# Layer 1 of a two-layer trunk with h's hi and lo parts joined in one matmul, and the context's residual added by DMA

## The chip, the cores and the metric

The kernel runs on one core of one Trainium2 chip. The metric is the device time of one execution in microseconds (us); of several runs the median is given. The engines are TensorE (PE, matmuls; PEld is its load of weights), VectorE (DVE), ScalarE (ACT), GpSimd (POOL) and SyncE (SP), which issues the DMAs.

## The reference

Two layers (DEPTH = 2) of a hybrid mixer work on 256 latent tokens and 256 context tokens of 2048 features, batch 1, all in float32:

```python
for l in range(DEPTH):
    shift, scale, gate = jnp.split(silu_c @ w_mod[l] + b_mod[l], 3, axis=-1)      # and _c from c_ctx
    h = rmsnorm(x, g_pre[l]) * (1.0 + scale[:, None]) + shift[:, None]            # h_c from ctx
    proj, proj_c = h @ w_in[l], h_c @ w_in[l]
    # columns of proj: a_u, a_v, a_g (512 each), b_q (1024), b_k, b_v (256 each), b_g (1024), c_x, c_g (512 each)
    y_a = chunk_gmlp(gelu(a_u), gelu(a_v), ...) * silu(a_g)
    y_b = attention(b_q, b_k, b_v, context's k and v, sink) * silu(b_g)
    y_c = fourier_mix(c_x, w_f, b_f) * silu(c_g)
    x_new = x + gate[:, None] * rmsnorm(concat(y_a, y_b, y_c) @ w_out[l], g_post[l])
    if not last: ctx = ctx + gate_c * rmsnorm(y_of_ctx @ w_out[l], g_post[l])
    x = x_new
```

The output is x, the latent stream. In layer 1, the last, the context matters only through its keys and values, so of the context only the columns b_k and b_v are computed there.

## The kernel before, in words

**Exact products.** A float32 product is made of three matmuls in the format fp32r: every operand is split into hi (the value cast to fp32r, on ACT) and lo (value less hi, on DVE), and `mm3` (lines 383 to 386) adds hi·hi, hi·lo and lo·hi in PSUM. The feature-major streams are kept as 16 tiles `hh[k]` and `hl[k]` of [128 features, 512], latents in columns 0 to 255 and context in 256 to 511.

**Weights.** `Stream` (lines 329 to 379) loads w_in and w_out in pieces of [128, 1024] ("halves") through SP into a ring `raw` of three, and splits each into `whi` (ACT, line 367) and `wlo` (DVE, line 368), rings of four, ahead of their use.

**Units.** `tunit(n)` (line 473) makes 128 output columns of the projection for n tokens: 16 k steps, each three matmuls with a [128, 128] piece of the weights as the stationary operand and h as the moving one. In layer 0 n is 512, in layer 1 it is 256 (latents), and 512 for the two k units. The start of a layer makes a_v (token-major, `start_av`) and the first two heads of a_u (`start_au`) with k outermost, while h of the next k tile is being made (`prep_h`, `make_h`, lines 445 to 459). Then come the units au2, au3, cx0 to cx3, ag0 to ag3, cg0 to cg3, k0, k1, then v, q0 to q7, bg0 to bg7, and the output projection: `out_proj` feature-major in layer 0, `finish` token-major in layer 1, with four column groups c, two token tiles t and 16 k steps.

**Order.** The order on PE is the order of the program text (`manual_schedule`). Work that goes to other engines and comes back to PE is written as generators: each is queued in `later` with delays in planned us, and `later.tick` runs it when as much planned matmul time has passed (YF between the stages of the C branch, YQ, YA and YB in attention, YX, YR and YH at the boundary, YT in the output projection). DVE, ACT, POOL and SP run in an order that a scheduler makes from the program's order and priorities; `low(n)` lowers a priority. Each of these engines takes its instructions strictly in that order.

**Modulation.** Silu(c) @ w_mod is summed on DVE for most columns, in steps of two [128, 512] products per 512 KB load into the ring `mraw` of two. `RATE` says how many steps go beside each phase of units (`pace`). The last of them is layer 1's gate (`mod_gate1`, lines 236 to 252): four accumulators of [128, 512], in the tiles ctrh, ctrl, nstrh and nstrl. `gate1` (lines 254 to 263) sums each over the partitions with ones on PE and applies b_mod and g_post, whose rows come by DMA into `mraw`.

**Boundary.** Between the layers, `boundary(s, acc)` (line 908) makes x1 = x0 + gate * y / rms(y) of a stream: the sums of squares in `acc` give r; every tile is multiplied by r on DVE, x0, loaded by SP into places of the ring `raw`, is added (DVE or POOL), and ACT squares the result. PE sums the squares with ones (line 944) to get the next 1/rms. The latents go first (s = 0, at the end of layer 0). The context (s = 1, `boundary_ctx`, line 980) runs beside the units of layer 1 from au3 on, with lowered priority; it then makes the context's h, 16 tiles in the order `ORDER`.

**Places in layer 1.** `ysl(k)`, the result of a branch, lies in the context half of `yo[k]`, so a gate that writes it must come after the context's h of tile k has been made (the assertion in `gate`). Products not yet gated lie in y1: the A branch's in the tile `vv`, the C branch's in kt0 and kt1.

Of the kernel before, what the change touches and what calls it, by code (L numbers as in the profile page):

```python
# [7 lines left out]
F32 = mybir.dt.float32  # L8
# [3 lines left out]
ALU = mybir.AluOpType  # L12
# [15 lines left out]
def units():  # L28
    """(name, first column, columns, first k tile, k tiles): blocks of w_in of 128 x 2048 each."""
# [37 lines left out]
def trunk_kernel(ctx: ExitStack, tc: tile.TileContext, xT, xhalf, cT, wss, wsl, wmod, win, wout0, wout1, const, vec, rows,  # L67
# [24 lines left out]
    # ---- constants  # L92
# [17 lines left out]
    class low:  # L110
        """instructions that may wait for the next `n`."""
# [22 lines left out]
    # ---- modulation: columns [128, 16, stream] of scale, shift and gate  # L134
# [5 lines left out]
    def mod_cols(l, cb, ps8):  # L140
        """ps8 [128, 4, 2]: silu(c) @ w_mod for 512 columns of column block cb."""
# [54 lines left out]
    def mod_dve(l, cb, red):  # L196
        """red [128, 2, 16]: sums over the 32 partitions of each quadrant, transposed."""
# [38 lines left out]
    def mod_gate1():  # L236
        """products of silu(c) and the gate's columns of w_mod in layer 1, still to be summed over partitions."""
# [16 lines left out]
    def gate1():  # L254
        """(sum + b_mod) * g_post of layer 1's gate, on all partitions."""
        for c in range(4):
            r = sb([P, 2, 512], F32, "mraw", 2)
            DMA.dma_start(r, rows[None, :, c * 512:(c + 1) * 512].to_broadcast([P, 2, 512]))
            ps = ms_ps("gate")
            PE.matmul(ps, ones, g1[c], start=True, stop=True)  # L260
            V.tensor_tensor(out=g1[c], in0=r[:, 0], in1=ps, op=ALU.add)
            V.tensor_tensor(out=g1[c], in0=g1[c], in1=r[:, 1], op=ALU.mult)
            yield YT

    def mod_rest():
# [3 lines left out]
        while "acc" not in state:  # L269
# [58 lines left out]
    # ---- weights: raw -> exact parts hi + lo, in halves of a unit, ahead of their use  # L328
# [59 lines left out]
    def part(w, c):  # L388
        """columns c of both parts; a part is a tile or a list of tiles side by side."""
# [19 lines left out]
    # ---- per-token reciprocal rms from sums over features  # L409
# [14 lines left out]
    def col_sums(ps, q, n, start=True, stop=True):  # L424
        """columns of ps: sums over the partitions of q [128, n * 128], one accumulation group."""
# [10 lines left out]
    # ---- streams in feature-major tiles  # L436
# [7 lines left out]

    def make_h(l, k, rb, streams):
        """h = x * rstd * gs + sh, as hi + lo; rb: rstd over the tokens of `streams`."""
# [6 lines left out]
        for s in streams:  # L453
            sl = slice(s * S, (s + 1) * S)
            first = A.activation(hh[k][:, sl], t[:, sl], AF.Identity, bias=sh[l][:, k, s:s + 1])  # L455
        for s in streams:
            sl = slice(s * S, (s + 1) * S)
            last = V.scalar_tensor_tensor(out=hl[k][:, sl], in0=t[:, sl], scalar=sh[l][:, k, s:s + 1],
                                          in1=hh[k][:, sl].bitcast(F32), op0=ALU.add, op1=ALU.subtract)
# [13 lines left out]
    def tunit(n, sl=None):  # L473
        """feature-major product of one unit of 128 columns: PSUM [128, n]."""
# [8 lines left out]
        return ps  # L483

# [610 lines left out]
```

## Time and profile before

| | |
|---|---|
| median of 3 runs | 1171.52 us (1169.95 to 1171.75) |
| span of the profiled execution, first to last instruction | 1167.9 us; of its time around the span nothing is listed, the median of the runs is 3.6 us above it |
| PE busy | 1136.0 us (97%) |
| DVE, ACT, POOL busy | 881.8, 509.8, 17.3 us |
| mean granted TensorE clock | 0.996 |
| start (modulation and layer 0's first products) | 0 to 137 us |
| layer 0's units and output projection | 137 to 757 us |
| layer 1's start (a_v, au0, au1) | 757 to 794 us |
| au2 to cg3, beside them the context's boundary | 794 to 891 us |
| k0, k1, then v | 891 to 936 us |
| q and bg units with attention | 936 to 1062 us |
| output projection and the end | 1062 to 1168 us |

Rows of a group read: line, engine, operation, out<-in by the program's names, shapes, count, then busy time in us and mean ns of one, then the engine's idle time just before these instructions and what ended most of it. Rows of the timeline read: start in us, duration in us, engine, line, operation, names, shapes, count, and in brackets idle time before it with what ended it. Matmuls overlap, so the distance of their starts is their cost. Rows of waits read: who waited for whom, total us, times, longest us. DMA rows give the issues, KB each and the median us from issue to landing.

### The profile page before, as it was taken

The page shows a single profiled execution, that of the slowest core. Times are in us where ns is not written, and L with a number is a line of the kernel's source. Part 1 is how long each engine was busy: PE and PEld are TensorE (multiplying, and loading weights), DVE is VectorE, ACT ScalarE, POOL GpSimd, SP SyncE. Part 2 cuts the span into 40 slices and gives each one's busy share as a digit, 9 for nine tenths or more (in the row PEclk, how much of TensorE's full clock was granted, in tenths as well). Part 3 has the DMA queues.
Part 4 walks back from the last instruction along what each step waited for, and adds up shares of the span by engine and source line. Part 5 has one row for each costly group of instructions (what it writes and reads, how often), then busy time and mean ns, then how long its engine had stood idle before and what let it go on. Part 6 is the DMA issues. An engine that isn't in the chain of part 4 may idle for free.

```text
span 1167.9 us, 17483 instructions
## 1 busy us (share of the span) xinstructions
PE 1136.0 (97%) x6656; PEld 953.7 (82%) x6656; DVE 881.8 (76%) x1469; ACT 509.8 (44%) x914; POOL 17.3 (1%) x23
## 2 busy tenths in 40 slices
PE   3999999999999999999999999999999999999996
PEld 1466688888898888888888888889899999997885
DVE  5454498888988878798989886495896678888554
ACT  4222513322224667632533233365563278745442
POOL 0000000000000000000000000200000000000001
PEclk9999999999999999999999999999999999999998
DMA  9999765466665334455466665365656665688563
GB/s 339 378 387 357 254 196 166 145 202 193 200 200 178 105 114 136 134 175 173 158 199 209 205 216 162 109 207 173 205 158 205 203 200 178 195 269 244 190 187 120
DMA packets 73892, 234.32 MB, mean 201 GB/s; under 512 B 8528, under 2 KB 9680, under 8 KB 73808
## 3 DMA queue, kind: packets, MB, share of 16 engines
q1 hardware_dynamic: 73808, 233.21, 61.6%
q8 instruction: 52, 0.85, 0.3%
q14 instruction: 32, 0.26, 0.1%
HBM read 231.08 MB, written 2.10 MB: 200 GB/s over the span
## 4 chain that ended last, share of the span: by engine, by line
PE 92%; DVE 3%; DMA 2%; ACT 2%; issue 1%; POOL 0%; SPq 0%; DVEq 0%; ACTq 0%; POOLq 0%
PE ps_t L384 20%; PE ps_t L385 20%; PE ps_t L386 20%; PE ps_mod L172 3%; PE ps_av L384 2%; PE ps_y L386 2%; PE ps_y L384 2%; PE ps_y L385 2%; PE ps_av L385 2%; PE ps_av L386 2%; PE ps_v L386 1%; PE ps_v L384 1%; PE ps_v L385 1%; PE ps_tp L722 1%; PE ps_au L384 1%
## 5 line engine op out<-in xcount | busy, mean ns | idle before, releaser
L384 PE MATMUL ps_t<-hh,whi 128*128 128x512 f32 (+1 forms) x1296 | 452.1, 349 | 0.0
L386 PE MATMUL ps_t<-hh,wlo 128*128 128x512 f32 (+1 forms) x1296 | 447.4, 345 | 0.0
L385 PE MATMUL ps_t<-hl,whi 128*128 128x512 f32 (+1 forms) x1296 | 447.0, 345 | 0.0
L367 ACT CAST whi<-raw 128x1024 fp32r<-128x1024 f32 x218 | 228.2, 1050 | 397.3 <-PE ps_t L385 274.4
L368 DVE TENSOR_TENSOR wlo<-raw,whi 128x1024 fp32r<-128x1024 f32 x218 | 265.3, 1220 | 99.1 <-ACT whi L367 98.8
L384 PEld LDWEIGHTS ps_t<-hh,whi 128*128 128x128 f32 x1296 | 244.9, 189 | 34.3 <-issue 4.6
L386 PEld LDWEIGHTS ps_t<-hh,wlo 128*128 128x128 f32 x1296 | 244.7, 189 | 30.6
L385 PEld LDWEIGHTS ps_t<-hl,whi 128*128 128x128 f32 x1296 | 244.9, 189 | 28.9 <-issue 0.5
L209 DVE SCALAR_TENSOR_TENSOR macc<-mraw,cs,macc 128x512 f32<-128x512 f32 x360 | 249.9, 745 | 17.6 <-DMA mraw<-in_wmod_dram 17.5
L455 ACT ACTIVATE hh<-w2k,sh 128x256 fp32r<-128x256 f32 x64 | 29.0, 502 | 61.4 <-DVE w2k L451 61.4
L384 PE MATMUL ps_y<-whi,hh 128*128 128x512 f32 x112 | 45.0, 401 | 0.0
L386 PE MATMUL ps_y<-whi,hl 128*128 128x512 f32 x112 | 43.8, 392 | 0.0
L385 PE MATMUL ps_y<-wlo,hh 128*128 128x512 f32 x112 | 43.7, 390 | 0.0
L384 PE MATMUL ps_av<-whi,hh 128*128 128x512 f32 x96 | 40.0, 416 | 0.0
L385 PE MATMUL ps_av<-wlo,hh 128*128 128x512 f32 x96 | 37.9, 395 | 0.4 <-DVE wlo L368 0.4
L172 PE MATMUL ps_mod<-hh,kt 128*32 128x512 f32 x64 | 21.5, 649 | 17.0 <-DMA hh<-in_wss_dram 17.0
L386 PE MATMUL ps_av<-whi,hl 128*128 128x512 f32 x96 | 37.6, 392 | 0.0
L386 PE MATMUL ps_v<-whi,hl 128*128 128x256 f32 x128 | 36.2, 283 | 0.0
L384 PE MATMUL ps_v<-whi,hh 128*128 128x256 f32 x128 | 36.2, 283 | 0.0
L385 PE MATMUL ps_v<-wlo,hh 128*128 128x256 f32 x128 | 36.2, 283 | 0.0
L468 DVE TENSOR_TENSOR acc<-acc,w2k 128x512 f32<-128x512 f32 (+1 forms) x33 | 21.2, 641 | 18.7 <-ACT w2k L467 17.2
L401 ACT CAST w2k<-ps_tp 128x512 fp32r<-128x512 f32 x40 | 23.5, 587 | 22.8 <-PE ps_scc L385 12.0
(292 smaller groups left out, 1491.8 us busy)
## 6 DMA issues: line engine op xcount, KB each, us to landing
raw<-in_win_dram SPq DMA_DIRECT2D x160, 512.0 KB, 4.1
mraw<-in_wmod_dram SPq DMA_DIRECT2D x128, 512.0 KB, 4.3
raw<-in_wout_dram SPq DMA_DIRECT2D x64, 512.0 KB, 4.2
hh<-in_wss_dram SPq DMA_DIRECT2D x32, 256.0 KB, 5.6
hl<-in_wss_dram SPq DMA_DIRECT2D x32, 256.0 KB, 5.4
yo<-in_xT_dram SPq DMA_DIRECT2D x16, 256.0 KB, 5.4
mraw<-in_wsl_dram SPq DMA_DIRECT2D x8, 512.0 KB, 6.9
yo<-in_wsl_dram SPq DMA_DIRECT2D x16, 256.0 KB, 7.2
```

The lines of the kernel that those rows point to most:

```text
L172: PE.matmul(ps[32 * kk:32 * kk + 32, 0:n], cpad[:, kg * 4 + kk], ws[kk], start=kg == 0, stop=kg == 3, tile_position=(0, 32 * kk))
L209: V.scalar_tensor_tensor(out=acc[:, s], in0=w[:, kk % 2], scalar=c, in1=acc[:, s], op0=ALU.mult, op1=ALU.add)
L367: A.copy(ph, r[:, c])
L368: self.last = V.tensor_tensor(out=pl, in0=r[:, c], in1=ph.bitcast(F32), op=ALU.subtract)
L384: PE.matmul(ps, st[0], mv[0], start=start, stop=False)
L385: PE.matmul(ps, st[0], mv[1], start=False, stop=False)
L386: PE.matmul(ps, st[1], mv[0], start=False, stop=stop)
L401: A.copy(hi, src)
L455: first = A.activation(hh[k][:, sl], t[:, sl], AF.Identity, bias=sh[l][:, k, s:s + 1])
L468: V.tensor_tensor(out=acc[:, sl], in0=acc[:, sl], in1=q[:, sl], op=ALU.add)
L722: PE.transpose(tp[:, (2 * j + b) * P:(2 * j + b + 1) * P], src, ident)
```

## The change

Five edits, all in layer 1 or at the boundary to it; the program of layer 0 stays as it is.

1. *Joined parts.* In layer 1 `hh[k]` holds the latents' h as [hi | lo], 512 columns, and `hl[k]` the context's in the same way. A k step of a latent unit is then two matmuls (`mm2`): the weights' hi with all 512 columns, the weights' lo with the 256 columns of hi, into one bank of PSUM. `joined` adds the two halves of the result: an ACT copy of one out of PSUM, a DVE addition of the other, into a tile of the ring `join` of two. The k units do this for both streams with two banks. What followed a unit (gates, rope, the C branch, gelu) reads the joined tile.
2. *Context's x0 by DMA.* `boundary_ctx` multiplies a tile by r on DVE, and then POOL issues a DMA that adds x0 from DRAM to it. Squares come six tiles later (LATE), on ACT; they are added up on DVE into acc, and the sums over the partitions are made at the end by the same few products as the first ones.
3. *A longer chain.* The context's h is made in the order 12 to 15, then 0 to 11, and planned delays change (YF of layer 1 from 3.8 and 3.4 to 6.0 and 5.2; YC, YE new).
4. *y of branch A apart.* The results of ag0 to ag3 stay in y1, now in the tile `macc`, so their gates no longer wait for the context's h.
5. *Gate sums at fixed places.* `gate1(c)` is called at four places of the output projection (GATES), with its rows in ws and bsb; the products of layer 1's gate go on in that stage (RATE: bg1 from 2.2 to 0.3, out1 new with 1.4).

```diff
-    YF = [5.0, 2.8], [3.8, 3.4]
+    YF = [5.0, 2.8], [6.0, 5.2]
...
-                k1=2.5, v1=2.5, q1=1, bg1=2.2)
+                k1=2.5, v1=2.5, q1=1, bg1=0.3, out1=1.4)
...
-    YT = 2.0
+    YT = 3.0
+    GATES = {4: 0}, {0: 1}, {0: 2, 14: 3}, {}
     YH = 2.0
-    NX = [4, 2]
-    YX, YR = [1.0, 2.0], 0.8
+    NX, LATE = 4, 6
+    YX, YR, YC, YE = 1.0, 0.8, 1.5, 5.0
...
+    def gate1(c):
+        r = [sb([P, 512], F32, tag) for tag in ("ws", "bsb")]
+        for i in range(2):
+            DMA.dma_start(r[i], rows[None, i, c * 512:(c + 1) * 512].to_broadcast([P, 512]))
+        ps = ms_ps("gate")
+        PE.matmul(ps, ones, g1[c], start=True, stop=True)
+        V.tensor_tensor(out=g1[c], in0=r[0], in1=ps, op=ALU.add)
+        V.tensor_tensor(out=g1[c], in0=g1[c], in1=r[1], op=ALU.mult)
...
+    def h_of(l, k, sl):
+        if l == 0:
+            return hh[k][:, sl], hl[k][:, sl]
+        s, a = sl.start // S, sl.start % S
+        t, b = (hh, hl)[s][k], a + sl.stop - sl.start
+        return t[:, a:b], t[:, S + a:S + b]
...
+    def mm2(ps, w, h, k):
+        PE.matmul(ps, w[0], h, start=k == 0, stop=False)
+        PE.matmul(ps[:, 0:S], w[1], h[:, 0:S], start=False, stop=k == KT - 1)
+
+    def joined(ps):
+        t = sb([P, S], F32, "join", 2)
+        A.copy(t, ps[:, S:T])
+        V.tensor_tensor(out=t, in0=t, in1=ps[:, 0:S], op=ALU.add)
+        return t
+
+    def tunit1(streams):
+        pss = [mm_ps("t") for _ in streams]
+        for k in range(KT):
+            if k % 8 == 0:
+                w = W.next()
+            for s, ps in zip(streams, pss):
+                mm2(ps, part(w, slice((k % 8) * P, (k % 8 + 1) * P)), (hh, hl)[s][k], k)
+                later.tick(PASS * S)
+        return [joined(ps) for ps in pss]
...
-        ysl = (lambda k: yo[k][:, S:T]) if last else (lambda k: yo[k])
+        ysl = (lambda k: y1[k] if k < 4 else yo[k][:, S:T]) if last else (lambda k: yo[k])
...
-            a = sb([P, 4, 256], F32, "vv")
+            a = sb([P, 4, 256], F32, "macc")
...
-            ps = tunit(n)
+            ps = tunit1([0])[0] if last else tunit(n)
...
-            ps = tunit(T)
+            pss = tunit1([0, 1]) if last else [tunit(T)]
...
-            assert not last or k in state["ctx"]
+            assert not last or k < 4 or k in state["ctx"]
...
-        later.add(gate1(), YT)
-        later.add(turn(), 2 * YT)
+        later.add(turn(), YT)
+        state["phase"] = "out1"
...
                 later.tick(PASS * 1024)
+                if k in GATES[c]:
+                    gate1(GATES[c][k])
...
+    def boundary_ctx(acc):
+        r = sb([P, S], F32, "rbs", 2)
+        r0 = yield from rms_of(1, acc[:, CTX], 3.2)
+        A.copy(r, r0)
+        acc1 = acc[:, CTX]
+        for k in range(KT + LATE):
+            if k < KT:
+                V.tensor_tensor(out=yo[k][:, CTX], in0=yo[k][:, CTX], in1=r, op=ALU.mult)
+                G.dma_start(yo[k][:, CTX], xhalf[1, k // 4][:, k % 4], accum_op=ALU.add)
+            i = k - LATE
+            if i >= 0:
+                q = w2k([P, S]) if i else acc1
+                A.activation(q, yo[i][:, CTX], AF.Square)
+                if i:
+                    V.tensor_tensor(out=acc1, in0=acc1, in1=q, op=ALU.add)
+            if k % 2:
+                yield YC
+        yield YE
+        r0 = yield from rms_of(1, acc1, 4.0)
+        r = sb([P, S], F32, "rbs", 2)
+        V.tensor_copy(r, r0)
+        for i, k in enumerate([12, 13, 14, 15] + list(range(12))):
+            make_h(1, k, r, [1])
+            state["ctx"].append(k)
+            if i % 2:
+                yield YH
```

`rms_of` is the first part of the old `boundary`: column sums of acc, the reciprocal root on POOL, and its broadcast by ones. The old `boundary` stays for the latents.

More of the change, by code (lines that the diff above doesn't have):

```diff
@@ L252, in mod_gate1 @@
             yield
[L254 to L263, printed above, removed]
+    def gate1(c):
[6 more added lines that the diff above has]
+        V.tensor_tensor(out=g1[c], in0=g1[c], in1=r[1], op=ALU.mult)
     def mod_rest():
@@ L787, in layer @@
         for h in range(8):
-            ps = tunit(n)
+            ps = tunit1([0])[0] if last else tunit(n)
             if h == 7:
@@ L822, in out_proj @@
             o_evac(j, ps, yo[j], acc, [0], False)
-        later.add(boundary(0, acc), 1.0)
+        later.add(boundary(acc), 1.0)
         for j in range(KT - HELD, KT):
@@ L906, in trunk_kernel, with rms_of, boundary @@
     rbs = {}
-    def boundary(s, acc):
-        sl = slice(s * S, (s + 1) * S)
+    def rms_of(s, acc, wait):
+        ps = ms_ps("rs")
+        col_sums(ps, acc, 2)
+        dg = rstd_diag(ps[:, 0:2], 2, D)
+        yield wait
+        return bcast(dg, 2)[:, 0:S]
+    def boundary(acc):
         x0s = []
@@ L978, in lowered, with after_start, prep_h @@
             yield d
-    def boundary_ctx():
-        yield from lowered(boundary(1, state["acc"]))
-        for i, k in enumerate(ORDER):
-            with low(LOWB):
-                make_h(1, k, rbs[1], [1])
-            state["ctx"].append(k)
-            if i % 2:
-                yield YH
+    def after_start(l):
+        if l == 1:
+            later.add(lowered(boundary_ctx(state["acc"])))
+    def prep_h(l, k):
+        new_h(k)
+        if l == 0:
+            return make_h(0, k, rb0, [0, 1])
+        return make_h(1, k, rbs[0], [0])
     with tc.manual_schedule(engines={mybir.EngineType.PE}):
```

70 lines of the change are left out of this document (30 added, 40 removed).

## The prediction

> **What bounds the kernel now.** I read the page's first and fourth parts, then the busy times by stage, then single stretches of TensorE.
>
> ```profile
> span 1167.9 us, 17483 instructions
> PE 1136.0 (97%) x6656; PEld 953.7 (82%) x6656; DVE 881.8 (76%) x1469; ACT 509.8 (44%) x914; POOL 17.3 (1%) x23
> ...
> PE 92%; DVE 3%; DMA 2%; ACT 2%; issue 1%; POOL 0%; SPq 0%; DVEq 0%; ACTq 0%; POOLq 0%
> ```
>
> TensorE (PE) is busy for 97% of the span, and 92% of the chain that ended last is its own work. So a change is worth what it takes out of PE's stream, less the waits that it puts in. Layer 1 is where the change lies; its stages (start and length, then busy time per engine with instruction counts, then granted clock, DMA share and GB/s):
>
> ```profile
> 794.00:891.00 97.00, 97.00 (x784) 91.58 (x783) 75.83 (x148) 53.75 (x104) 2.09 (x3) 1.00 0.58 175
> 891.00:913.00 22.00, 22.00 (x99) 18.16 (x98) 14.13 (x21) 6.73 (x12) 0.00 (x0) 1.00 0.67 215
> 913.00:936.00 23.00, 23.00 (x193) 22.98 (x192) 13.87 (x21) 7.29 (x13) 0.00 (x0) 1.00 0.67 211
> 936.00:1020.00 84.00, 82.11 (x639) 78.97 (x638) 69.99 (x128) 65.56 (x131) 0.00 (x0) 1.00 0.60 191
> 1020.00:1062.00 42.00, 42.00 (x356) 42.00 (x355) 36.94 (x56) 21.46 (x38) 0.00 (x0) 1.00 0.82 265
> 1062.00:1082.00 20.00, 18.92 (x83) 13.81 (x82) 15.27 (x28) 10.88 (x20) 0.00 (x0) 1.00 0.74 234
> ```
>
> These are: units au2 to cg3 with the context's boundary beside them; the two k units; v; the q units with attention (the stretch ends inside the gates of B); the rest of those gates; and the start of the output projection. PE idles only in the q stage (84.00 less 82.11) and at the output's start (20.00 less 18.92). Everywhere else its time is the sum of its matmuls.
>
> **Part A: joined h_hi and h_lo.** Each k step of a latent unit had three matmuls of 256 columns; it gets one of 512 (both halves under the weights' hi) and one of 256. What matters is the distance between starts, not the duration of one, since matmuls overlap.
>
> ```profile
> 950.28 0.28 PE L385 MATMUL ps_t<-hl,whi 128*128 128x256 f32 x1
> ...
> 952.90 0.28 PE L386 MATMUL ps_t<-hh,wlo 128*128 128x256 f32 x1
> ```
>
> Between these two lie 22 distances: 2.62 / 22 = 0.119 us each, so a step costs 0.357. (The v stage agrees: 23.00 / 193 = 0.119.) For a mixture of 512 and 256 the trace has the start of layer 1, where six av matmuls of 512 alternate with six au matmuls of 256:
>
> ```profile
> 766.36 0.40 PE L384 MATMUL ps_av<-whi,hh 128*128 128x512 f32 x1
> ...
> 767.75 0.28 PE L384 MATMUL ps_au<-hh,whi 128*128 128x256 f32 x1
> ...
> 768.46 0.40 PE L384 MATMUL ps_av<-whi,hh 128*128 128x512 f32 x1
> ```
>
> One period is 2.10 us for six of each: 0.350 per pair. The step saves 0.007 us. There are 30 latent units of 16 steps (au2, au3, four cx, four ag, four cg, eight q, eight bg) and 32 steps of au0 and au1, 512 in all: **−3.8 us**. Its ends: nothing, if changing widths at every matmul costs what the wider matmul saves; and, if the 256 then took half of the period's 512 (1.39 / 6 = 0.232, half 0.116, a pair 0.348 and, with the k stage's 22.00 / 99 = 0.222 for the 512, 0.338), 0.019 × 512 = −9.7. I take the measured period, the nearest row.
>
> The k units serve both streams. Three matmuls of 512 per step become two pairs: 32 steps × 0.700 = 22.4 us where the stage had 22.00: **+0.4**. The v and av products keep their sizes.
>
> **Part B: the context's sums.** Before, 16 squares went through ones on PE, two at a time:
>
> ```profile
> 814.13 0.28 PE L386 MATMUL ps_t<-hh,wlo 128*128 128x256 f32 x1
> 814.34 0.63 PE L944 MATMUL ps_rs<-w2k,ones 128*32 128x256 f32 x4
> 814.90 0.38 PE L384 MATMUL ps_t<-hh,whi 128*128 128x256 f32 x1
> 815.12 0.28 PE L385 MATMUL ps_t<-hl,whi 128*128 128x256 f32 x1
> ```
>
> Such a visit takes 0.56 us and stretches the matmul before it to 0.21 and the one behind it to 0.22, each from 0.119: 0.75 in all. Eight visits in the 794 to 891 stage: −6.0. What closes them changes too: the two products with the selector go, and a second set of column sums over acc comes, as the first one stands in the trace:
>
> ```profile
> 843.31 0.50 PE L952 MATMUL ps_rs<-cst,w2k 128*128 128x1 f32 x4
> 843.67 0.36 PE L384 MATMUL ps_t<-hh,whi 128*128 128x256 f32 x1
> ...
> 808.12 0.28 PE L427 MATMUL ps_rs<-zero,ones 128*128 128x2 f32 x2
> 808.26 0.58 PE L429 MATMUL ps_rs<-ones,acc 128*128 128x1 f32 x4
> 808.71 0.36 PE L384 MATMUL ps_t<-hh,whi 128*128 128x256 f32 x1
> ```
>
> 0.36 goes, 0.59 comes: +0.2. **Part B is −5.8.** On VectorE (DVE) 16 additions of x0 go and 15 additions of squares come; even. SP loses four loads of x0, 512 KB each, which also took places in the raw ring; POOL gets 16 accumulating DMAs of 128 KB. ACT's squares then wait for those landings, and behind each on ACT's queue stand casts of weights. ACT has room there:
>
> ```profile
> ACT whi L367 <- PE ps_t L385: 274.4, 99, 6.3
> L934 POOL TENSOR_TENSOR yo<-yo,raw 128x256 f32<-128x256 f32 x8 | 6.8, 850 | 4.2 <-DVE yo L933 3.8 <-ACT yo L804 0.2
> out_dram<-yo SPq DMA_DIRECT2D x4, 128.0 KB, 1.9
> w2k<-in_const_dram SPq DMA_DIRECT2D x2, 128.0 KB, 4.5
> ```
>
> A weight cast waits 2.8 us on average for PE to free a buffer, so a late square first uses that up, and then up to three halves of weights (8 steps × 0.350 = 2.8 us each) that lie ready. No row shows a DMA issued by POOL. Bounds per DMA: 0.85 us of POOL (its x0 addition) and 1.9 us of landing; or the 4.5 us landing with nothing overlapped. I take the first, the nearest row of POOL and of a DMA of this size, and cost it at nothing; the other end is a rival below.
>
> **Part C: the gate of layer 1 moved.** Of its products on DVE, 22 instructions stood in the bg stage; now two do, and 23 come in the output projection. The bg stage loses 20 × 0.75 = 15 us of DVE's 36.94, but PE had no idle time there, so this yields nothing. At the output's start it does:
>
> ```profile
> L247 DVE SCALAR_TENSOR_TENSOR nstrl<-mraw,cs,nstrl 128x512 f32<-128x512 f32 x15 | 11.2, 749 | 4.6 <-DMA mraw<-in_wmod_dram 4.4
> 1082.00:1152.00 70.00, 70.00 (x317) 57.36 (x317) 35.80 (x40) 31.62 (x44) 0.00 (x0) 1.00 0.55 169
> 1070.33 0.66 PE L847 MATMUL ps_x<-identr,yo 128*128 128x128 f32 x4 [0.72 <-DVE ctrh L261]
> 1079.02 0.55 PE L847 MATMUL ps_x<-identr,yo 128*128 128x128 f32 x3 [0.36 <-DVE nstrh L261]
> mraw<-in_rows_dram SPq DMA_DIRECT2D x4, 512.0 KB, 6.3
> ```
>
> The four gate sums stood there within 13 us, each behind a load of rows that lands after 6.3 us, and the transposes of x1 waited for their PSUM: 0.72 + 0.36. Spread over the projection, with the rows loaded into ws and bsb ahead, this goes: **−1.1**. The 23 × 0.75 = 17 us lie in a stage where DVE has 34 of 70 us free and DMA 45%; no cost. If that cover were gone, the weights' lo parts would come late and PE would wait by DVE's excess. On SP the rows of the first gate now wait until attention has read the k parts in ws and bsb; behind them stand weight loads, but those scores are whole units older. Nothing.
>
> **Part D: the added joining.** Each unit gets an ACT copy and a DVE addition of 256 columns out of PSUM, 36 of each:
>
> ```profile
> 987.60 0.37 ACT L730 COPY yo<-ps_o 128x256 f32<-128x256 f32 x1 [0.17 <-PE ps_o L386]
> L652 DVE TENSOR_TENSOR w2k<-ps_t,cst 128x256 f32<-128x256 f32 x20 | 8.5, 424 | 19.6 <-ACT mgl L650 19.5
> 991.12 0.42 DVE L402 TENSOR_TENSOR w2k<-mgl,w2k 128x256 fp32r<-128x256 f32 x1
> 993.64 0.39 PE L384 MATMUL ps_sc<-kt,w2k 128*128 128x512 f32 x1
> PE ps_o L385 <- DVE w2k L402: 1.7, 3, 1.0
> ```
>
> Each chain behind a unit gets 0.37 + 0.42 = 0.79 us longer. In gates nobody waits for it, and the C branch gets 2.2 and 1.8 more in its two planned delays. In the q stage the delay stays: there q's lo part ends at 991.54 and the scores start at 993.64, 2.1 later, so this head can pay. But the stage is where DVE (69.99 of 84) and ACT (65.56) are fullest; eight joins add 3.4 and 3.0, and PE already waits 1.7 there for P's lo part. Ends: −1.7 (all waits go, as PE's stream shifts) and 8 × 0.79 = +6.3 (every head exposed). I take **+1.0**, about half of the present wait again.
>
> **Sum.** −3.8 + 0.4 − 5.8 − 1.1 + 1.0 = −9.3 us on the profiled 1167.9, so a span of 1158.6. The runs' median, 1171.5, is 3.6 above that span; with the same 3.6 around it: **1162.2 us**.
>
> **Rivals.**
> 1. *Columns alone count.* A step streams 768 columns before and after; if the time went by columns, part A is 0: 1166.0. Against it: 256 columns take 0.119, and 512 take 0.222 to 0.232 and not 0.238. Chance 0.10. The Trainium skill (TensorE: Matmul & The Clock Gate, Back-to-back issue gap) gives N / 2.4 + 2.5 ns between warm matmuls: 3 × 109.2 against 215.8 + 109.2, an estimate of 2.6 ns a step, and by it part A would be −1.3 and the time 1164.7. The trace's 119 ns for 256 columns at full clock does not agree with its 109.
> 2. *More is won.* Part A at 0.016 a step (0.341 a pair, between its ends), −8.2, and q's wait of 1.7 gone: −8.2 + 0.4 − 5.8 − 1.1 − 1.7 = −16.4, 1155.1. Speaks for it that a whole 512 hides the next weight load. Chance 0.10.
> 3. *The joins eat it.* Every q chain exposed, 6.3 instead of 1.0, and the four C chains 4 × 0.79 = 3.2: 1162.2 + 5.3 + 3.2 = 1170.7, no change. For it: both engines over 80% in that stage with the join. Against it: the 2.1 us of slack. Chance 0.09.
> 4. *Slower: POOL's DMAs in a row.* PE's second column sums stand in ag1, fixed in its order, about 69 steps of 0.350 and some 5 us of C products after the first product with r: 29 us; some 5 of those go on the last landing and the last additions. PE waits once 16 DMAs take over 24 us, 1.5 each, and the change loses all from (24 + 9.3) / 16 = 2.1 each. At 3 us (between 0.85 and 4.5) it is 48 − 24 = 24 late: 1186. Against it: POOL is idle and its only rows are under 2 us. Chance 0.14. The Trainium skill (DMA: Bandwidth & Descriptors, Anatomy of one DMA — SWDGE (gpsimd) path) puts a fixed 2.0 us on such a DMA, most of it the receipt of the write; by that, issues overlap and this rival does not come. No run here shows it yet.
>
> The forecast has the remaining 0.57.
>
> **Range and chances.** A measurement of this kernel can tell about 0.2% from no change: 1169.2 to 1173.9 is the same. The forecast and rivals 1 and 2 are faster: 0.57 + 0.10 + 0.10 = 0.77; rival 3 is the same, 0.09, of which the edges give one part to slower: 0.08; slower is rival 4 and that part, 0.15. The range goes from rival 2's 1155 to 1175, so that the upper half of rival 4 and little else is left out.
>
> **What would show it.** Step A: starts 0.350 apart per pair of 512 and 256 in the q and bg units. Step B: no visits of 32 columns between au2 and k beyond boundary 0's; no wait at the second column sums. Step C: transposes at the output's start without idle time. Step D: waits of the scores or of P's lo part in the q stage of about 2.7 us. Wrong it would be by a PE idle time over 3 us anywhere between 800 and 900 (POOL's landings) or in the q stage (joins), or by pairs of 0.357.

## The result, and the profile after

The changed kernel takes **1157.91 us** (median of four runs, 1156.94 to 1160.56) where the kernel before took 1171.63 beside it: a ratio of 0.9886, 95% interval 0.9870 to 0.9902. The forecast was 1162.2, with a range of 1155 to 1175. The profiled execution took 1158.18 us, its span is 1156.4. These are the page's span, busy times and chain that ended last:

```profile
span 1156.4 us, 16569 instructions
...
PE 1126.6 (97%) x6146; PEld 927.1 (80%) x6146; DVE 893.5 (77%) x1503; ACT 520.0 (45%) x950; POOL 31.7 (3%) x39
...
PE 95%; DMA 2%; DVE 1%; ACT 1%; issue 0%; SPq 0%; POOL 0%; DVEq 0%; POOLq 0%; ACTq 0%
```

TensorE still sets the time: the span is 11.5 us shorter and PE's busy time 9.4. Its share of the chain went from 92% to 95%, so waits went as well as work. DVE and ACT have more to do than before, 11.7 and 10.2 us. The busy times of layer 1's stages after, at the places that answer to the six stages shown of before (start and length, then PE, PEld, DVE, ACT, POOL, then PE's granted clock, DMA share, GB/s):

```profile
793.00:886.00 93.00, 92.34 (x546) 80.75 (x545) 80.18 (x162) 60.21 (x122) 17.37 (x19) 1.00 0.68 188
886.00:907.00 21.00, 21.00 (x121) 18.27 (x120) 14.98 (x24) 6.55 (x12) 0.00 (x0) 1.00 0.67 221
907.00:930.00 23.00, 23.00 (x193) 22.95 (x193) 14.54 (x22) 7.88 (x14) 0.00 (x0) 1.00 0.65 209
930.00:1010.00 80.00, 80.00 (x484) 70.66 (x484) 69.57 (x133) 67.75 (x139) 0.00 (x0) 1.00 0.59 192
1010.00:1052.00 42.00, 42.00 (x258) 37.33 (x257) 29.27 (x47) 25.51 (x50) 0.00 (x0) 1.00 0.56 174
1052.00:1072.00 20.00, 20.00 (x95) 16.15 (x94) 17.77 (x31) 11.37 (x19) 0.00 (x0) 1.00 0.70 236
```

In the q stage (930 to 1010) PE has no idle time left, though DVE's busy share rose from 83% to 87%. At the output's start (1052 to 1072) its 1.08 us of idle time are gone too.

For the comparison of many kernels I cut each trace at starts of PE's matmuls in layer 1 and took the distances in us. "Units" runs from the last matmul of a_v to the first of v: the last 0.9 us of layer 1's start, then au2 to the end of the k units. "q, bg" runs from the last matmul of v to the first of the output projection and holds all q and bg units with attention. "Output" is the output projection up to its last matmul. The start of layer 1 and the v stage differ by at most 0.4 between any two kernels here. Each row comes from one profiled execution; where an edit leaves a stage alone, it repeats well: q and bg take 121.7 to 121.8 and the output 95.9 to 96.5 in the changed kernel and in the four below that differ from it only in the units.

| kernel (span) | units | q, bg | output |
|---|---|---|---|
| before (1167.9) | 120.3 | 126.3 | 96.4 |
| after (1156.4) | 114.4 | 121.7 | 95.9 |
| difference | −5.9 | −4.6 | −0.5 |
| forecast by the terms | −7.1 | −0.9 | −1.1 |

That the time lies within the range is in part luck: two stages (units, output) gave less than forecast, and one (q, bg) gave far more. The experiments below are about these differences.

### The profile page after: what moved, and what is told of

The parts are those of the page before. It is cut to its first block, busy times and chain, and to the rows that moved or that the text cites. A ratio compares the mean times of both kernels' runs of the same rounds, so it can differ in the third digit from the quotient of the medians.

```text
span 1156.4 us, 16569 instructions
## 1 busy us (share of the span) xinstructions
PE 1126.6 (97%) x6146; PEld 927.1 (80%) x6146; DVE 893.5 (77%) x1503; ACT 520.0 (45%) x950; POOL 31.7 (3%) x39
## 4 chain that ended last, share of the span: by engine, by line
PE 95%; DMA 2%; DVE 1%; ACT 1%; issue 0%; SPq 0%; POOL 0%; DVEq 0%; POOLq 0%; ACTq 0%
PE ps_t L384 15%; PE ps_t L385 15%; PE ps_t L386 15%; PE ps_t L496 11%; PE ps_t L497 5%; PE ps_mod L172 3%; PE ps_y L385 2%; PE ps_y L386 2%; PE ps_av L384 2%; PE ps_y L384 2%; PE ps_av L385 2%; PE ps_av L386 2%; PE ps_tp L759 1%; PE ps_v L386 1%; PE ps_v L384 1%; PE ps_v L385 1%
## 5 line engine op out<-in xcount | busy, mean ns | idle before, releaser
L384 PE MATMUL ps_t<-hh,whi 128*128 128x512 f32 (+1 forms) x784 | 301.0, 384 | 0.0
L386 PE MATMUL ps_t<-hh,wlo 128*128 128x512 f32 (+1 forms) x784 | 299.4, 382 | 0.0
L385 PE MATMUL ps_t<-hl,whi 128*128 128x512 f32 (+1 forms) x784 | 299.1, 382 | 0.0
L496 PE MATMUL ps_t<-hh,whi 128*128 128x512 f32 x512 | 185.6, 400 | 0.0
L385 PEld LDWEIGHTS ps_t<-hl,whi 128*128 128x128 f32 x784 | 147.4, 188 | 27.3 <-issue 0.2
L497 PE MATMUL ps_t<-hh,wlo 128*128 128x256 f32 x512 | 143.5, 280 | 0.0
L463 ACT ACTIVATE hh<-w2k,sh 128x256 fp32r<-128x256 f32 x48 | 21.7, 501 | 56.6 <-DVE w2k L459 56.6
```

What stands on the lines that cost most here:

```text
L384: PE.matmul(ps, st[0], mv[0], start=start, stop=False)
L385: PE.matmul(ps, st[0], mv[1], start=False, stop=False)
L386: PE.matmul(ps, st[1], mv[0], start=False, stop=stop)
L463: first = A.activation(h_of(l, k, sl)[0], t[:, sl], AF.Identity, bias=sh[l][:, k, s:s + 1])
L496: PE.matmul(ps, w[0], h, start=k == 0, stop=False)
L497: PE.matmul(ps[:, 0:S], w[1], h[:, 0:S], start=False, stop=k == KT - 1)
```

## The experiments

Times are medians in us, parts of a kernel come from its profiled execution; ratios are to the kernel before on the same chip, with their 95% intervals. All kernels compute the whole result.

### One part undone at a time

**The joining.** Each k step is three matmuls of 256 columns again; nothing else changes.

```diff
-                mm2(ps, part(w, slice((k % 8) * P, (k % 8 + 1) * P)), (hh, hl)[s][k], k)
+                t = (hh, hl)[s][k]
+                mm3(ps[:, 0:S], part(w, slice((k % 8) * P, (k % 8 + 1) * P)), (t[:, 0:S], t[:, S:T]), k == 0, k == KT - 1)
...
-        return [joined(ps) for ps in pss]
+        return [ps[:, 0:S] for ps in pss]
```

> The changed kernel with the joining alone undone: latent units, au0, au1 and the k units of layer 1 make three matmuls of 256 columns per k step again (h still lies as [hi | lo]), and nothing is added up behind a unit. Theory 1 (the joined step is shorter by what the starts show, 0.357 to 0.351; the q stage's waits for P's lo part went because the gate's products were moved): 512 steps x 0.0065 = +3.3 and 64 k steps x 0.0065 = +0.4, so +3.7 against the changed kernel's 1157.9, about 1161.6, and the wait of ps_o in the q stage stays near zero. Theory 2 (the join itself took that wait away, since rope reads SBUF and PSUM comes free sooner): the same +3.7 and the wait of 2.7 us back, about 1164.3. Theory 3 (the joins cost the q stage what they add): less than +3.7, down to nothing.

Measured 1170.63, ratio 0.9995 (0.9985 to 1.0006): all of the gain is gone, far more than any of the three theories said. Units 115.6, q and bg 126.4, output 101.1. These are its waits of PE in the q and bg units, then those in the output projection, then PE's rows around the longest of them:

```profile
PE ps_o L385 <- DVE w2k L402: 2.2, 3, 1.0
```

```profile
PE ps_y L384 <- ACT whi L367: 2.5, 1, 2.5
PE ps_y L385 <- DVE tot L906: 0.9, 1, 0.9
```

```profile
1137.33 0.79 PE L384 MATMUL ps_y<-whi,hh 128*128 128x512 f32 x1 [2.51 <-ACT whi L367]
1139.01 0.80 PE L385 MATMUL ps_y<-wlo,hh 128*128 128x512 f32 x1 [0.89 <-DVE tot L906]
1139.61 0.63 PE L386 MATMUL ps_y<-whi,hl 128*128 128x512 f32 x1
1140.03 0.63 PE L384 MATMUL ps_y<-whi,hh 128*128 128x512 f32 x1
...
1144.45 0.39 PE L384 MATMUL ps_y<-whi,hh 128*128 128x512 f32 x1
1144.67 0.39 PE L385 MATMUL ps_y<-wlo,hh 128*128 128x512 f32 x1
```

The wait for P's lo part in the q stage is back with the three matmuls, so the joining had taken it away, as theory 2 had it. The output projection is 5.2 us longer too, though the joining does nothing there: the cast of a weight comes late, and for 4 us after the wait the matmuls start 0.43 apart and last 0.63, instead of 0.23 and 0.39. ACT's casts of weights wait for loads of w_out there. These are the waits from 1075 to 1160, first after the change, then without the joining:

```profile
ACT whi L367 <- DMA raw<-in_wout_dram: 7.7, 5, 3.0
```

```profile
ACT whi L367 <- DMA raw<-in_wout_dram: 19.8, 11, 4.3
```

Before the change these casts waited 0.5 us for loads in the whole output projection and 30.3 for PE to free a buffer, so weights lay ready. The gate's products were moved into this stage, and each two of them need a load of 512 KB. Why the loads come later still without the joining is not shown.

**The gate's part.** Sums one after the other at the output's start, all products ahead of it, as before.

```diff
-                k1=2.5, v1=2.5, q1=1, bg1=0.3, out1=1.4)
+                k1=2.5, v1=2.5, q1=1, bg1=2.2)
...
-        later.add(turn(), YT)
+        later.add(gate1(), YT)
+        later.add(turn(), 2 * YT)
```

> The changed kernel with the gate's part alone undone: products of layer 1's gate at the old rates (bg1 2.2, none in the output projection), gate sums one behind the other at the output's start, rows into mraw, YT 2.0. Theory 1 (moved products freed the q stage): the wait of ps_o of 2.7 us returns and the output's start loses 0.6 to 1.1, together +3.3 to +3.8, about 1161.5. Theory 2 (the join took the wait away): +0.6 to +1.1 alone, about 1158.8.

Measured 1169.22, ratio 0.9984 (0.9975 to 0.9994). That is 7.7 us more than the higher of the two forecasts. Units 114.6, q and bg 122.1, output 106.1: 10.2 us longer than with the change, most of it in one wait of 8.7; behind that wait the granted clock was 0.55 from 1067 to 1073. Its wait of PE around there, SP's rows in that time, and the busy times of the bg stage:

```profile
PE ps_x L884 <- DVE ctrh L260: 8.7, 1, 8.7
```

```profile
1049.19 10.77 SPq L358 DMA_DIRECT2D raw<-in_wout_dram  x4
1061.40 1.95 SPq L257 DMA_DIRECT2D mraw<-in_rows_dram  x2
```

```profile
1010.00:1052.00 42.00, 42.00 (x256) 37.28 (x255) 38.55 (x62) 25.82 (x50) 0.00 (x0) 1.00 0.81 274
```

DVE is busy for 38.55 of 42 us (92%), against 29.27 after the change. The products of the gate end at 1062.9, but PE reaches the first gate sum at 1054.0; the rows, which share the ring mraw with the loads of the products, are issued at 1061.40 only. Before the change the products ended at 1058.3 and PE came at 1065.0. So once the joins are in, the products must leave this stage, or PE waits 9 us for them.

**The context's squares on PE again** (x0 still by POOL's DMA), and, apart, **x0 by SP and DVE again** (sums as changed).

```diff
-                if i:
-                    V.tensor_tensor(out=acc1, in0=acc1, in1=q, op=ALU.add)
+                    PE.matmul(cs_ps[c, 0:S], ones[:, 0:32], q, start=nsq[0] < 4, stop=nsq[0] >= KT - 4,
+                              tile_position=(0, 32 * (nsq[0] % 4)))
```

> The changed kernel with the context's squares summed again on TensorE, two per visit, and closed by two products with the selector; x0 still added by POOL's DMA. Theory B (the gain of the context's part is TensorE's time): eight visits of 0.75 less 0.2, +5.8, about 1163.7, with PE's ps_rs time up by 4.2 and its neighbours by 1.5. Rival (the gain is DVE's, or SP's raw ring): at most +2, about 1160.

```diff
-                G.dma_start(yo[k][:, CTX], xhalf[1, k // 4][:, k % 4], accum_op=ALU.add)
+                V.tensor_tensor(out=yo[k][:, CTX], in0=yo[k][:, CTX], in1=x0s[k // 4][:, k % 4], op=ALU.add)
```

> The changed kernel with the context's x0 loaded by SP into the raw ring (four loads of 512 KB) and added on DVE, all else as changed. Theory B (only the sums on TensorE counted; the DMA adds nothing and costs nothing): 0 within 1 us of 1157.9; ACT's wait of 4.7 us for landings goes without effect. Rival (taking the additions from DVE mattered): DVE gets 16 x 0.42 = 6.7 us in a stage of 93 where it is busy for 80.2, and PE waits for up to that: to 1164.6.

Measured 1170.66, ratio 1.0001 (0.9986 to 1.0016), and 1165.30, ratio 0.9949 (0.9933 to 0.9966). Only the units differ from the changed kernel: 126.8 and 121.0 instead of 114.4. PE's waits between au2 and v, first for the squares on PE, then for x0 by SP:

```profile
PE ps_rs L1018 <- ACT w2k L1011: 2.2, 1, 2.2
PE ps_rs L1026 <- DVE w2k L1022: 1.3, 1, 1.3
```

```profile
PE ps_rs L429 <- DVE acc L1023: 2.1, 1, 2.1
PE ps_t L496 <- ACT whi L367: 1.8, 1, 1.8
PE ps_t L497 <- DVE wlo L368: 1.1, 2, 0.8
```

The squares on PE cost 12.3 us, twice the 5.8 of the matmuls: PE also waits for them, 3.5 in the two lines, and behind each of these waits its granted clock is lower (0.64 from 828 to 832, 0.62 from 849.5 to 854). With x0 by SP and DVE the units are 6.6 longer. That is as much as the work of the sixteen additions on DVE (6.6 us, in a stage where DVE was busy for 80.18 of 93), but the two lines with `ps_t` are waits for weights: the four loads of x0 take places in the ring `raw` again, ACT's casts of weights wait 4.5 us for loads where they waited for none in the changed kernel, and the clock behind is 0.57 from 838 to 842. The experiment doesn't part DVE's work from these loads. The prediction had put the additions that DVE loses and gets as even, which they are in work; only both moves together gave PE its time.

### One part alone

If each part's gain were its own, the three alone would add up to the whole.

**The joining alone**, on the kernel before (one of the places where units are made):

```diff
-            ps = tunit(n)
+            ps = tunit1([0])[0] if last else tunit(n)
```

> The kernel before with the joining alone (512 and 256 columns per step, copy and addition after each unit); context, gate sums and planned delays as before. Theory 1 (parts add): the steps give 3.8, the k units cost 0.4, the wait in the q stage goes with 2.7: 1171.6 - 6.1 = 1165.5; if the two short delays of the C branch show the joins, up to 3.2 more, 1168.7. By the forecast's own terms (joins cost 1.0 in q): 1169.2. Rival (parts need each other): what the steps save is waited for elsewhere, above all in the output projection: 1170.5 to 1172.5.

**The gate's part alone**, on the kernel before (the rates and the places of the sums; `gate1` is that of the change):

```diff
-                k1=2.5, v1=2.5, q1=1, bg1=2.2)
+                k1=2.5, v1=2.5, q1=1, bg1=0.3, out1=1.4)
...
+                if k in GATES[c]:
+                    gate1(GATES[c][k])
```

> The kernel before with the gate's part alone: products of layer 1's gate in the output projection, gate sums at four fixed places. Theory 1 (parts add): the waits of the transposes go, 0.5 to 1.1 us: 1170.5 to 1171.1. Rival (parts need each other): the output projection now holds 17 us more of DVE and its loads, with nothing else changed: weights come late there by 2 to 5 us: 1173 to 1176.

**The context's part alone**, the changed kernel with both other parts undone (its order, delays and places stay):

> The changed kernel without the joining and with the gate's part as before: the context's part is what is left (sums, x0 by DMA, order, longer delays, results of branch A apart). Theory 1 (parts add, by the terms): 5.8 forecast for the sums, 4.7 seen in au2 to k: 1165.8 to 1167. Rival (undoings add): the two single undoings cost 12.7 and 11.3 us, most of that waits at and in the output projection; if both losses come, 1157.9 + 24 = 1182; if one hides the other, about 1170.

| kernel | time | ratio (interval) | units | q, bg | output |
|---|---|---|---|---|---|
| joining alone | 1179.64 | 1.0068 (1.0050 to 1.0086) | 124.9 | 122.6 | 106.4 |
| gate alone | 1173.85 | 1.0024 (1.0013 to 1.0035) | 120.3 | 126.1 | 100.7 |
| context alone | 1165.85 | 0.9953 (0.9938 to 0.9969) | 115.6 | 126.3 | 98.3 |
| all but the joining | 1170.63 | 0.9995 (0.9985 to 1.0006) | 115.6 | 126.4 | 101.1 |
| all but the gate | 1169.22 | 0.9984 (0.9975 to 0.9994) | 114.6 | 122.1 | 106.1 |
| all | 1157.91 | 0.9886 (0.9870 to 0.9902) | 114.4 | 121.7 | 95.9 |

The parts do not add up: alone they give +0.68%, +0.24% and −0.47%, together −1.14%. Two of them make the kernel slower by themselves. For the joining none of the forecasts reached its 1179.64; the gate's part came as its rival said, and only the context's part as the theory that parts add. The joining with the gate's part on the old boundary was not run. Read down the columns and it becomes plain which needs which:

- *q, bg*: 121.7 to 122.6 with the joining, 126.1 to 126.4 without. Here the joining gives its 3.8 to 4.7 whatever else is done.
- *Units*: the joining costs 4.6 with the old boundary (124.9 against 120.3) and gives 1.0 to 1.2 with the new one. With the old boundary PE waits 2.2 us for the broadcast of r, and its clock is 0.62 from 849.5 to 854. The experiment doesn't part the new delays of the C branch from the rest of the context's part.
- *Output*: with the joining, moving the gate gives 10.2 (95.9 against 106.1); without it the move costs 2.9 (101.13 against 98.25) to 4.3 (100.7 against 96.4).

PE's longest wait of the joining alone in the output projection is the one of the gate's sum seen above:

```profile
PE ps_x L884 <- DVE ctrh L261: 9.9, 1, 9.9
```

### Why the wait in the q stage went

The joins add 0.79 us to each head's chain, and the wait shrank. The rows of ACT around the cast of q's hi part (`w2k<-mgl`) and the exponentials of the head before (`es`, then `w2k<-ps_sc`), first before the change, then after:

```profile
1000.23 0.41 ACT L401 CAST w2k<-mgl 128x256 fp32r<-128x256 f32 x1 [1.36 <-DVE mgl L654]
1000.55 0.29 ACT L687 ACTIVATE es<-nm,skb 128x2 f32<-128x2 f32 x1
```

```profile
971.82 0.29 ACT L724 ACTIVATE es<-nm,skb 128x2 f32<-128x2 f32 x1
972.02 0.39 ACT L401 CAST w2k<-mgl 128x256 fp32r<-128x256 f32 x1
```

And ACT's waits for the rotated q over the whole q stage, before and after:

```profile
ACT w2k L401 <- DVE mgl L654: 7.3, 7, 1.8
```

```profile
ACT w2k L401 <- DVE mgl L691: 1.0, 1, 1.0
```

Before, in the last six heads, the cast waits for DVE in five of them, 0.7 to 1.4 us each; the two exponentials of the scores always stand behind it and wait too, and in four heads `es` as well. So the softmax is late, and P's lo part with it. After, `es` comes first in five of the six heads and the cast then finds its operand ready; in the one head where it still comes first it waits 0.97. The program's order of these instructions is the same; the scheduler placed them otherwise, presumably since q is ready later with the joining. Two experiments on the kernel without joining test this. The first gives the old order more time:

```diff
-    YQ, YA, YB = [5.5, 6.0], [10.0, 8.0], [3.8, 4.0]
+    YQ, YA, YB = [5.5, 6.0], [10.0, 8.0], [3.8, 5.0]
```

> The changed kernel without the joining (as in the run before of that name, 1170.6 us), and with one planned delay of attention longer: 1.0 us more of other matmuls between the transposes of P and the products of its second half. Theory (slack): the joining took the wait for P's lo part away only because it shifted the order on ACT and DVE, so 1 us of planned time does the same: waits for P's lo under 0.5 us, q and bg stage 2.0 to 2.7 us shorter than without the joining, total 1168 to 1169. Rival (load): ACT and DVE are late as such, the chain just moves with the delay and the wait stays or turns up at the next head: stage within 0.5 us, total 1170 to 1171.

Measured 1177.36, ratio 1.0050 (1.0032 to 1.0068). The wait for P's lo part grew from 2.2 to 6.1, and q and bg took 133.9. So slack was not what was missing; but the rival's "within 0.5 us" failed too. Part of these 7 us more is a clock of 0.57 behind two of the waits (977 to 981 and 1001 to 1005); the profiled execution, 1180.31, was the slowest of four. In the trace of this kernel ACT's casts of q wait up to 3.0 us for DVE, and three of them 2.1 to 3.5 for PE, again with the exponentials behind them:

```profile
ACT w2k L401 <- DVE mgl L692: 6.1, 4, 3.0
```

The second leaves TensorE's order as it is and makes q's cast, with the lo part behind it, 1.2 planned us later and behind `es`; in the trace the scores' exponentials never stand behind the cast then:

```diff
-            rope(*q, ps)
-            yield YQ[l]
+            rot = rope(*q, ps, late=last)
+            if last:
+                yield 1.2
+                with tc.issue_after(exps[-1].ins) if exps else low(0):
+                    A.copy(q[0], rot)
+                V.tensor_tensor(out=q[1], in0=rot, in1=q[0].bitcast(F32), op=ALU.subtract)
+            yield YQ[l] - (1.2 if last else 0)
```

> The changed kernel without the joining (1170.6 us), with one change of order on ACT: the cast of q's hi part is made 1.2 planned us later and stands behind the exponentials of the head before, as it does with the joining; TensorE's order is the same. Theory (order on ACT): the joining's gain in the q stage came from this order, so the wait for P's lo part goes here too: its waits from 2.2 to under 0.5 us, the q and bg stage 2.0 to 2.8 us shorter than without the joining (126.4 to about 124), total 1168 to 1169 if the output projection stays. Rival (the joining itself, by freeing PSUM or by its reads of SBUF): the wait stays at 1.5 to 2.5 and the stage within 0.5 us, total 1170 to 1171.

Measured 1169.60, ratio 0.9988 (0.9978 to 0.9999). PE's waits in the q and bg units:

```profile
PE ps_o L385 <- DVE w2k L402: 0.5, 1, 0.5
PE ps_sc L384 <- ACT w2k L709: 0.5, 1, 0.5
```

That is 1.0 less than without the joining, nearer to the order theory's 1168 to 1169 than to the rival's 1170 at least. The wait for P's lo part fell from 2.2 to 0.5 without any joining, as the order theory said. The stage got only 0.7 shorter (125.7), since 0.5 came back at the scores and 0.6 in the matmuls of the units. The output projection was 2.2 longer, in an execution that was the slowest of ten (1171.6). So the order on ACT explains that wait, 1.8 of the 2.8 us by which the products with P differ between the two kernels; that the whole difference of the stage comes from it is not shown, and the order made here is not quite the one that the joining brings, which leaves the exponentials behind the cast and the cast without a wait.

### When POOL's DMAs would be too slow

Rival 4 said that PE waits once the 16 DMAs take over 24 us. Cutting each into two and four makes more issues of the same bytes:

```diff
-                G.dma_start(yo[k][:, CTX], xhalf[1, k // 4][:, k % 4], accum_op=ALU.add)
+                for e in range(n):
+                    es = slice(e * S // n, (e + 1) * S // n)
+                    G.dma_start(yo[k][:, S + e * S // n:S + (e + 1) * S // n], xhalf[1, k // 4][:, k % 4, es], accum_op=ALU.add)
```

> The changed kernel with each of POOL's 16 accumulating DMAs cut into two of 64 KB. Rival 4's rule (the DMAs go one after the other on POOL, and TensorE waits at the second column sums once they take over 24 us): at the measured 0.9 us of issue each, 32 x 0.9 = 29 us, about 5 late: 1163 us, with a wait of 4 to 6 us at the second sums. If an issue's time goes by its bytes, 32 x 0.45 = 14.4 us: no wait, 1158.

> The changed kernel with each of POOL's 16 accumulating DMAs cut into four of 32 KB. At 0.9 us of issue each, 64 x 0.9 = 58 us: about 34 late at the second column sums, and TensorE waits there for most of that: 1185 to 1192 us. If an issue's time goes by its bytes: no wait, 1158.

One run each: 1165.29 and 1192.06; only the units are longer, 122.0 and 149.1 instead of 114.4. POOL's issues and their landings, as changed, then in two, then in four:

```profile
L1007 POOL DMA_DIRECT2D yo<-in_xhalf_dram x16 | 14.4, 1761 | 9.3 <-DVE yo L1006 8.5 <-DVE join L503 0.7
yo<-in_xhalf_dram POOLq DMA_DIRECT2D x16, 128.0 KB, 7.9
```

```profile
L1009 POOL DMA_DIRECT2D yo<-in_xhalf_dram x32 | 29.0, 2784 | 4.4 <-DVE yo L1006 4.4
yo<-in_xhalf_dram POOLq DMA_DIRECT2D x32, 64.0 KB, 6.1
```

```profile
L1009 POOL DMA_DIRECT2D yo<-in_xhalf_dram x64 | 58.0, 4147 | 4.4 <-DVE yo L1006 4.4
yo<-in_xhalf_dram POOLq DMA_DIRECT2D x64, 32.0 KB, 6.4
```

An issue holds POOL for 0.90 us whatever its bytes (14.4 / 16, 29.0 / 32, 58.0 / 64). Against the 24 us of cover, 58.0 is 34 over, and the units are 34.7 longer; 29.0 is 5 over and costs 7.5. So PE pays about the excess, as the rule says, but neither the place nor the way is the rule's: with four pieces PE's waits in the units add up to 27, and behind them its clock is 0.52 to 0.59 (831 to 838, 853 to 864, 874 to 880), so that the match of 34 and 34.7 is in part luck. PE's longest waits with four pieces, and what ACT waited for:

```profile
PE ps_f L384 <- ACT w2k L401: 14.7, 2, 10.7
PE ps_rs L429 <- DVE acc L1015: 8.0, 1, 8.0
PE ps_z L384 <- ACT w2k L401: 3.8, 1, 3.8
```

```profile
ACT w2k L1013 <- DMA yo<-in_xhalf_dram: 33.9, 13, 4.6
```

PE stops at the C branch's products first: their casts stand on ACT's queue behind squares that wait for POOL's landings, and the second column sums get only the rest, 8.0.

### A regrouped step

Four matmuls of 512, then four of 256, so that the width changes twice in four steps and not eight times:

```diff
+                    for ww, h, i in todo:
+                        PE.matmul(ps, ww[0], h, start=i == 0, stop=False)
+                    for ww, h, i in todo:
+                        PE.matmul(ps[:, 0:S], ww[1], h[:, 0:S], start=False, stop=i == KT - 1)
```

> The changed kernel with the matmuls of four k steps grouped: four of 512 columns, then four of 256. Theory (a change of width costs something): distances in the traces are 0.228 from 512 to 512, 0.233 from 512 to 256, 0.119 from 256 to 256, 0.117 from 256 to 512; a group of four then takes 3 x 0.228 + 0.233 + 3 x 0.119 + 0.117 = 1.391, 0.348 a step instead of 0.3505: 512 x 0.0027 = 1.4 us faster, 1156.5. Rival (only the sum of the columns counts): same, 1157.9. A shift of a few matmuls can change what the other engines' order meets, as the single undoings showed: then up to 4 us slower.

Measured 1163.44, ratio 0.9937 (0.9919 to 0.9955), slower than the changed kernel's 0.9886 and by 5.5 us where up to 4 had been allowed for. A group's starts:

```profile
1035.45 1.08 PE L516 MATMUL ps_t<-hh,whi 128*128 128x512 f32 x4
1036.36 0.64 PE L518 MATMUL ps_t<-hh,wlo 128*128 128x256 f32 x4
1036.83 1.09 PE L516 MATMUL ps_t<-hh,whi 128*128 128x512 f32 x4
```

From 1035.45 to 1036.83 lie 1.38 us, 0.345 a step in this group. Over all of layer 1's units the medians are 0.232 from 512 to 512 and 0.118 from 256 to 256, which gives 0.350; the 0.228 that I took came from layer 0. The matmuls of the q and bg units take 90.4 us against 90.8, so at most 0.0016 a step is won: changing widths costs next to nothing here. Most of the loss, 4.3, is in the output projection (100.2), where again a weight comes late and the clock behind is lower (0.76 from 1131 to 1138):

```profile
PE ps_y L384 <- ACT whi L367: 2.1, 1, 2.1
```

No kernel tried here is faster than the changed one.

## Why the prediction was right, and where it was not

- **What bounds the kernel** was right: the gain is PE's work and PE's waits.
- **Part A** was right in size (its own rows give 3.7 for the 3.8 of its sum). After the change pairs of starts lie 0.35 apart:

```profile
975.10 0.40 PE L496 MATMUL ps_t<-hh,whi 128*128 128x512 f32 x1
975.33 0.28 PE L497 MATMUL ps_t<-hh,wlo 128*128 128x256 f32 x1
975.45 0.39 PE L496 MATMUL ps_t<-hh,whi 128*128 128x512 f32 x1
```

  In the q and bg units the 256 steps take 1.9 us less than before, 0.0074 each. Rival 1 falls with it, and so does part A of rival 2 (0.016 a step); its other half, that q's wait goes, came true, and its 1155.1 lies nearer to the measured 1157.9 than the forecast does. By the formula that the Trainium skill gives (TensorE: Matmul & The Clock Gate, Back-to-back issue gap) for an isolated gap a step saves 0.0025, an estimate, a third of that; the measured 0.119 and 0.232 decide. The k units cost 0.7 instead of 0.4.
- **Part B** came out a little smaller. The context's sums took 5.4 us of PE's starts before and 1.2 after. In the units 5.9 were won where the terms said 7.1; of the missing 1.2, a new wait in the C branch is 0.7 and the k units are 0.3.
- **Part C** gave 0.5 instead of 1.1: the waits of the transposes went, and a new one of 0.8 for `tot` came. The step that cost its 17 us of DVE at "nothing" held only with the joining as changed: in three kernels with the move (without the joining, alone, regrouped) the output projection lost 2.9 to 4.3 us, with a late weight as its longest wait. It looked at DVE's free time, and what ran short was the lead of the weights' loads (waits of 0.5 us before, 7.7 and 19.8 in the lines above). What the working also missed is the other side: the bg stage could not have kept the products beside the joins, so with the joining the move is worth 10.2 in the output projection.
- **Part D** failed, in sign: +1.0 forecast, −2.7 measured in the products with P (15.3 to 12.6 us). "This head can pay" looked at the 2.1 us between q's lo part and its scores and priced the joins as added length. The lower end, −1.7 for "all waits go", was named and not taken, and is itself short. The runs put a change of order on ACT in its place for 1.8 of the 2.8 us between the kernels with and without the joining; the cause of the rest is open. A sum of durations shows no change of order.
- **Rival 3** fell: no head's scores waited. **Rival 4** did not come because an issue took 0.90 us, near the lower bound of 0.85 that was taken; with more issues PE did wait, by about the excess over 24 us, but not first at the second sums. In its sentence on the Trainium skill (DMA: Bandwidth & Descriptors, Anatomy of one DMA — SWDGE (gpsimd) path) the issues overlap with the landing, and the trace agrees: 14.4 us of issues beside landings of 7.9 each. Its fixed 2.0 us for one such DMA is far from those 7.9, and the measurement decides.

The sum was 2.2 us short: −9.3 forecast, −11.5 measured. Part D is 3.7 of it, and parts B, C and the k units give 1.8 back; the rest is 0.5 at most in any stage (the end behind the last matmul of the output projection). So the sum came close because errors of both signs met in it. The forecast of the time was 4.3 too long; the other 2.1 come from the 3.6 us that it set between span and median. In each execution for which both are known the device time is about 1.8 us above the span (after: 1158.18 and 1156.4), so the profiled execution of before, with its 1167.9, was by this estimate some 1.9 us faster than that kernel's median of 1171.6.

## What to carry to other kernels

In a kernel whose engines run in fixed queues, price a change by stage and by what each queue holds, not only by durations: here two of three parts were losses alone, and most of the gain came only when one part emptied the stage that another filled. A wait of PE can cost some 2 us more than its length, since the clock was lower behind most of the longer ones here. A chain can get shorter though an operation is added to it, if an instruction then stands behind others instead of blocking them, so look at which instruction waits at the head of its queue. Undo one part and do one part alone before crediting any of them.

## What the runs showed of the hardware

- After a stall of 2.5 us and another of 0.9 the matmuls of 512 started 0.427 apart for 4 us instead of 0.227, so the wait cost some 2 us more than its length. Most of PE's other waits of 1.8 us or more in these kernels were followed by a lower clock too, but not all: behind one of 2.7 in the kernel with the context's part alone the clock stayed at 1.00 (1066 to 1071), and behind the one of 2.1 with x0 by SP too (849.5 to 853.5). So the length of the wait alone doesn't decide it; what does is open. The stall of 0.8 in the changed kernel's output projection was followed by no such rows. In the kernel with all but the joining the granted clock from 1137 to 1147 was 0.67:

```profile
1137.00:1147.00 10.00, 8.78 (x27) 6.72 (x28) 5.81 (x13) 3.60 (x7) 0.00 (x0) 0.67 0.37 106
```

- An accumulating DMA of POOL holds POOL for 0.90 us on average whether it moves 32, 64 or 128 KB, and lands 6.1 to 7.9 us after its issue (medians; POOL's own record of the issue lasts 1.8 to 4.1 of them on average), where the output's 128 KB stores by SP took 1.9.
